# A hybrid decoder trunk in split float32 on one core: low parts of the weights last in every chunk, and the split by whole-chunk instructions on two engines

## The chip, the core and the metric

The kernel runs as one program on one core of a Trainium2 chip. The metric is the device time of one execution in microseconds. Three runs of the kernel before took 1512.72, 1508.36 and 1509.54 us, median 1509.54 us. The rows below come from one further execution that was taken with the hardware profiler.

The engines are named as in the profile: PE is TensorE (matmuls), PEld its weight loads, DVE is VectorE, ACT is ScalarE, POOL is GpSimd, and SP is SyncE, whose queue issues nearly all loads.

## The reference

Two layers on 256 tokens of 1024 channels, in float32:

```python
x = x + pool_mixer(rmsnorm(x), pool_w, pool_scale)          # layer 0
x = x + swiglu(rmsnorm(x), w_gate, w_up, w_down)            # 1024 -> 2816 -> 1024
x = x + ssd_mixer(rmsnorm(x), ...)                          # layer 1: Mamba2 SSD, 2048 inner channels
x = x + moe_swiglu(rmsnorm(x), w_router, ...)               # 8 experts, top 2, 1024 -> 3584 -> 1024
return rmsnorm(x, final_norm_w)

def swiglu(t, w_gate, w_up, w_down):
    return matmul(silu(matmul(t, w_gate)) * matmul(t, w_up), w_down)
```

Nearly all of the bytes are weights, and of these most belong to the eight experts (8 x 3 x 1024 x 3584 float32 numbers).

## The kernel before

**Split products.** A float32 number x is split exactly into a high part `hi` (x rounded to the type float32r) and a low part `lo = x - hi`. A product of two float32 matrices is then three float32r products that accumulate in one PSUM tile: high by high, high by low and low by high. So every weight is used by PE three times as 1024 or 512 columns of moving data: twice as its high part (with the activations' high and low parts) and once as its low part (with the activations' high part).

**The stream of weights.** The class `Stream` holds a list of 404 chunks in the order of their use, almost all of 1 MB (128 partitions x 2048 numbers). Line 80 issues a chunk's load on SP's queue as soon as a unit (a 1 MB buffer) is free. `ahead` splits a chunk: ACT copies it into the high part's unit (line 96), and VectorE subtracts that from the raw chunk into the low part's unit (line 99). Each chunk is split in two halves of 1024 columns, so by two instructions on ACT and two subtractions. `pool_every` gives the second half's subtraction of every n-th chunk to POOL: of every chunk in the pool mixer, of none in the dense SwiGLU, of every second in most of the SSD layer, and of every third from the SSD's output product to the end. `look` says how many chunks ahead of its use a chunk is split: two in most of the kernel, so `next()` of chunk c puts the split of chunk c + 2 into the queues of ACT and DVE, before whatever the program adds there afterwards. Chunks whose weights are scaled by a column (`scale`, the SSD's output product) take lines 102 and 103.

**Stages.** The pool mixer and the start of the dense SwiGLU (0 to about 50 us), the dense SwiGLU (to about 250 us), the SSD layer with the router (to about 490 us), the eight experts (to about 1490 us), and the last scatter and final norm. In the expert stage there are 56 blocks, seven for each expert, and a block takes six chunks: two of the gate product, two of the up product (`gmm`, lines 996 to 998: per chunk 4 k tiles of three products with 512 columns) and two of the down product (`D_part`, which calls `rows_mm`, line 276: per chunk 2 k tiles of six products with 512 columns). Between gate and up stand four transposes (line 1030); line 1011 is the gate's silu on ACT, 1024 the product with the up half on DVE, 238 and 239 the split of the hidden activations. At an expert's end come line 987 (two on DVE) and four additions of line 975, with eight products on PE.

**Order.** The program fixes the order of instructions on each engine by hand (`manual_schedule`); an engine takes its queue in order, so an instruction that waits holds all behind it. The waits are found by the framework from the tiles that an instruction reads and writes.

Of the kernel before, what the change touches and what calls it, by code (L numbers as in the profile page):

```python
# [40 lines left out]
class Stream:  # L41
    """The weights in the order of their use: loads that run ahead as far as free units allow, and
    the exact split of each float32 chunk into two float32r parts a few chunks before its products."""

    def __init__(self, nc, unit, chunks):
# [7 lines left out]
        self.pool_every = 0  # L53
# [30 lines left out]
    def ahead(self, to):  # L84
        while self.ns < min(to, len(self.chunks)):
# [40 lines left out]
def trunk_kernel(ctx, tc, x, cols, bands, cbf, rows, dskip, poolw, dgate, dup, ddown, wdt, wxbc, wz, wout,  # L126
# [114 lines left out]
    def norm(t, w, junk, add):  # L241
        """the residual's update (in halves) and its rmsnorm, for a token tile."""
# [9 lines left out]
    def norm_T(t, junk, th, tl):  # L252
        """the normed token tile transposed and split: [d, k, t] in two parts."""
# [7 lines left out]
    def wst(ps, wh, wl, f, xh, xl, ks):  # L261
        """channel-major product: weights stationary, both token tiles moving."""
        n = len(ks)
        for i, k in enumerate(ks):
# [7 lines left out]
    def rows_mm(acc, lh, ll, wh, wl, start, stop, hs=(0, 1)):  # L272
        """token-major product with one k tile of weights [128, 1024] moving."""
        for a, w, first, last in ((lh, wh, start, False), (lh, wl, False, False), (ll, wh, False, stop)):
            for h in hs:
                mm(acc[h], a, w[:, h * 512:(h + 1) * 512], start=first, stop=last)  # L276
                if between:
                    between.pop(0)()
# [998 lines left out]
```

## Time and profile before

| what | value |
|---|---|
| runs | 1508.36, 1509.54 (median), 1512.72 us |
| span of the profiled execution, first to last instruction | 1505.8 us, 19848 instructions (no time around it is listed) |
| PE busy | 1451.1 us (96%) |
| DVE, ACT, POOL busy | 1235.6 (82%), 1004.9 (67%), 428.0 us (28%) |
| granted TensorE clock, mean | 0.993 |
| read from HBM | 426.45 MB |

A matmul's end is modelled in the profile and matmuls overlap, so PE's busy time is no measure of its best pace; that is read from the distance between the starts of matmuls. An idle row such as `PE a L997 <- DVE u L99: 21.3, 29` means: PE stood idle 21.3 us in 29 places just before a matmul of line 997, and what ended it was DVE's instruction of line 99.

### The profile page before, as it was taken

Reading aid. Unit: us, or ns where it says so; the run is one execution under the profiler, and the core shown is the slowest. Engines: PE = TensorE matmul, PEld = TensorE weight load, DVE = VectorE, ACT = ScalarE, POOL = GpSimd, SP = SyncE. Lnnn points to the kernel's source line nnn. Section 1 sums busy time; section 2 is a strip of 40 time slices with the busy share of each in tenths; the row PEclk is TensorE's granted clock in tenths of the full one; section 3 lists DMA queues with packets and bytes.
Section 4 is the critical chain, followed back from the end, with each engine's and each line's share of the span. In section 5 each row is a group of like instructions: output and inputs, shape, how many; then the busy total and the mean of one; then the engine's idle time right before and its main releaser. Section 6 shows DMA issues by size and latency. Waiting matters only on the chain. (4 is left out here: it accounts for less than half of the span.)

```text
span 1505.8 us, 19848 instructions
## 1 busy us (share of the span) xinstructions
PE 1451.1 (96%) x7533; PEld 1215.1 (81%) x7534; DVE 1235.6 (82%) x1157; ACT 1004.9 (67%) x1248; POOL 428.0 (28%) x208
## 2 busy tenths in 40 slices
PE   7999999899999999999999999999999999999997
PEld 6999989899887787778877787888877777777775
DVE  7554557997767999998888899798898979889996
ACT  6443445766656777776776777777777667767775
POOL 3100004443223343232332333333323222332231
PEclk9999999999999999999999999999999999999998
DMA  8655365424456999888999998899998789999950
GB/s 339 253 184 180 109 240 211 140 79 146 168 203 276 351 360 362 306 334 311 383 360 350 351 342 323 319 368 376 351 351 331 305 348 360 355 343 342 342 211 30
DMA packets 60439, 428.87 MB, mean 285 GB/s; under 512 B 6832, under 2 KB 6960, under 8 KB 9008
## 3 DMA queue, kind: packets, MB, share of 16 engines
q1 hardware_dynamic: 59760, 425.94, 73.7%
q10 hardware_dynamic: 576, 1.59, 0.3%
q8 instruction: 61, 1.00, 0.3%
q14 instruction: 42, 0.34, 0.1%
HBM read 426.45 MB, written 1.05 MB: 284 GB/s over the span
## 5 line engine op out<-in xcount | busy, mean ns | idle before, releaser
L99 DVE TENSOR_TENSOR u<-u 128x1024 fp32r<-128x1024 f32 x665 | 943.2, 1464 | 177.5 <-ACT u L96 109.9
L96 ACT ACTIVATE u<-u 128x1024 fp32r<-128x1024 f32 x789 | 780.5, 1053 | 214.8 <-issue 40.1
L99 POOL TENSOR_TENSOR u<-u 128x1024 fp32r<-128x1024 f32 x124 | 353.2, 2849 | 731.1 <-ACT u L96 441.6
L997 PE MATMUL a<-u 128*128 128x512 f32 x896 | 355.6, 397 | 22.5 <-DVE u L99 21.3
L996 PE MATMUL a<-u 128*128 128x512 f32 x896 | 356.0, 397 | 0.0
L998 PE MATMUL a<-u 128*128 128x512 f32 x896 | 351.8, 393 | 0.0
L276 PE MATMUL b<-u,q 128*128 128x512 f32 x1344 | 319.2, 392 | 3.4 <-DVE u L99 3.4
L276 PEld LDWEIGHTS b<-u,q 128*128 128x128 f32 x1344 | 251.1, 188 | 60.3 <-DVE u L99 6.0
L997 PEld LDWEIGHTS a<-u 128*128 128x128 f32 x896 | 168.5, 188 | 73.7 <-DVE u L99 36.2
L998 PEld LDWEIGHTS a<-u 128*128 128x128 f32 x896 | 168.2, 188 | 36.8
L996 PEld LDWEIGHTS a<-u 128*128 128x128 f32 x896 | 168.3, 188 | 36.0
L266 PE MATMUL b<-u 128*128 128x256 f32 x584 | 166.7, 286 | 3.0 <-ACT u L96 3.0
L268 PE MATMUL b<-u 128*128 128x256 f32 x584 | 166.1, 284 | 1.1 <-DVE u L99 0.9
L267 PE MATMUL b<-u 128*128 128x256 f32 x584 | 165.9, 284 | 0.0
L266 PEld LDWEIGHTS b<-u 128*128 128x128 f32 x584 | 112.7, 193 | 3.9 <-ACT u L96 3.4
L268 PEld LDWEIGHTS b<-u 128*128 128x128 f32 x584 | 112.6, 193 | 1.5 <-DVE u L99 1.5
L267 PEld LDWEIGHTS b<-u 128*128 128x128 f32 x584 | 112.8, 193 | 0.5
L1011 ACT ACTIVATE q<-a,s 128x512 f32<-128x512 f32 x56 | 38.4, 685 | 55.5 <-PE a L998 55.5
L276 PE MATMUL a<-u,q 128*128 128x512 f32 x264 | 62.1, 391 | 0.7 <-ACT q L238 0.7
L276 PEld LDWEIGHTS a<-u,q 128*128 128x128 f32 x264 | 48.8, 188 | 10.6 <-ACT q L238 0.9
L597 DVE SCALAR_TENSOR_TENSOR q<-pad,col,q 128x256 f32<-128x256 f32 x96 | 55.3, 641 | 0.2
L515 POOL TENSOR_SCALAR nega<-nega 128x1 f32<-128x1 f32 x1 | 0.2, 245 | 192.6 <-ACT nega L514 192.6
(262 smaller groups left out, 1124.9 us busy)
## 6 DMA issues: line engine op xcount, KB each, us to landing
u<-in_mgate SPq DMA_DIRECT2D x112, 1024.0 KB, 6.9
u<-in_mup SPq DMA_DIRECT2D x112, 1024.0 KB, 6.9
u<-in_mdown SPq DMA_DIRECT2D x111, 1024.0 KB, 6.7
u<-in_wxbc SPq DMA_DIRECT2D x16, 1024.0 KB, 4.8
u<-in_dgate SPq DMA_DIRECT2D x11, 1024.0 KB, 4.9
u<-in_dup SPq DMA_DIRECT2D x11, 1024.0 KB, 7.3
u<-in_ddown SPq DMA_DIRECT2D x11, 1024.0 KB, 4.8
u<-in_wz SPq DMA_DIRECT2D x8, 1024.0 KB, 4.8
```

The lines of the kernel that those rows point to most:

```text
L96: self.nc.scalar.activation(hi[:, c], raw[:, c], AF.Copy)
L99: eng.tensor_sub(lo[:, c], raw[:, c], hi.bitcast(F32)[:, c])
L266: mm(ps, wh[:, k, c], xh[:, k], start=i == 0, stop=False)
L267: mm(ps, wh[:, k, c], xl[:, k], start=False, stop=False)
L268: mm(ps, wl[:, k, c], xh[:, k], start=False, stop=i == n - 1)
L276: mm(acc[h], a, w[:, h * 512:(h + 1) * 512], start=first, stop=last)
L515: pool.tensor_scalar(nega, nega, -1.0, None, op0=ALU.mult)
L597: dve.scalar_tensor_tensor(r[:, c], pad[:, c, 1 + k:1 + k + T], w[c][k], r[:, c], op0=ALU.mult, op1=ALU.add)
L996: mm(ps, a, wh[:, k], start=i == 0 and k == 0, stop=False)
L997: mm(ps, a, wl[:, k], start=False, stop=False)
L998: mm(ps, b, wh[:, k], start=False, stop=i == 1 and k == 3)
L1011: act(sil, ps, AF.Silu, scale=pair[e // 2].g[:, e % 2, 1:2])
```

## The change

Two things change together. First, in `wst`, `rows_mm`, `z_tile` and `gmm` the products with the high part of a chunk's weights come first for all k tiles of the chunk, and those with the low part last. `rows_mm` now takes all k tiles of a chunk at once, and `by_half` applies to a whole chunk. Second, an unscaled chunk is split by one instruction of 2048 columns on ACT and one on DVE; `pool_every` goes away, and with it POOL's part in the split. Line numbers in the new file are one to four lower or up to five higher.

```diff
             hi, lo = self.get([P, n], F32R), self.get([P, n], F32R)
-            for p, s in enumerate(range(0, n, D)):
-                c = slice(s, s + D)
-                if scale is None:
-                    self.nc.scalar.activation(hi[:, c], raw[:, c], AF.Copy)
-                    on_pool = p == 1 and self.pool_every and i % self.pool_every == 0
-                    eng = self.nc.gpsimd if on_pool else self.nc.vector
-                    eng.tensor_sub(lo[:, c], raw[:, c], hi.bitcast(F32)[:, c])
-                else:
-                    w = scale[s // D]
+            if scale is None:
+                self.nc.scalar.activation(hi, raw, AF.Copy)
+                self.nc.vector.tensor_sub(lo, raw, hi.bitcast(F32))
+            else:
+                for p, s in enumerate(range(0, n, D)):
+                    c, w = slice(s, s + D), scale[p]
...
-        for i, k in enumerate(ks):
-            c = slice(f * P, (f + 1) * P)
             mm(ps, wh[:, k, c], xh[:, k], start=i == 0, stop=False)
             mm(ps, wh[:, k, c], xl[:, k], start=False, stop=False)
+        for i, k in enumerate(ks):
             mm(ps, wl[:, k, c], xh[:, k], start=False, stop=i == n - 1)
...
+    def rows_mm(acc, tiles, start, stop, by_half=False):
+        n = len(tiles)
+        ops = []
+        for i, (lh, ll, wh, wl) in enumerate(tiles):
+            ops += [(lh, wh, start and i == 0, False), (ll, wh, False, False)]
+        for i, (lh, ll, wh, wl) in enumerate(tiles):
+            ops.append((lh, wl, False, stop and i == n - 1))
+        for hs in ((0,), (1,)) if by_half else ((0, 1),):
+            for a, w, first, last in ops:
+                for h in hs:
+                    mm(acc[h], a, w[:, h * 512:(h + 1) * 512], start=first, stop=last)
...
             for k in range(4):
-                a, b = pr.h[:, 4 * i + k, s], pr.l[:, 4 * i + k, s]
-                mm(ps, a, wh[:, k], start=i == 0 and k == 0, stop=False)
-                mm(ps, a, wl[:, k], start=False, stop=False)
-                mm(ps, b, wh[:, k], start=False, stop=i == 1 and k == 3)
+                mm(ps, pr.h[:, 4 * i + k, s], wh[:, k], start=i == 0 and k == 0, stop=False)
+                mm(ps, pr.l[:, 4 * i + k, s], wh[:, k], start=False, stop=False)
+            for k in range(4):
+                mm(ps, pr.h[:, 4 * i + k, s], wl[:, k], start=False, stop=i == 1 and k == 3)
...
-    st.reserve, st.look, st.pool_every = 2, 2, 3
+    st.reserve, st.look = 2, 2
```

On PE, in one chunk of an expert's gate product before (u_5499 and u_5500 are the chunk's high and low parts, u_4545 and u_4546 the activations' high and low parts):

```order
L996 MATMUL a_5519<-u_5499,u_4545 128x512 [waits Activation_49]
L997 MATMUL a_5519<-u_5500,u_4545 128x512 [waits DVE_49]
L998 MATMUL a_5519<-u_5499,u_4546 128x512
...
L996 MATMUL a_5519<-u_5499,u_4545 128x512 [waits Activation_49]
L997 MATMUL a_5519<-u_5500,u_4545 128x512 [waits Pool_49]
L998 MATMUL a_5519<-u_5499,u_4546 128x512
```

The first low part is read by the chunk's second product, that of the second half by its eighth. The same place in the changed kernel (u_6245 and u_6246 are the chunk's parts, u_5884 and u_5885 the activations'):

```order
L995 MATMUL a_6263<-u_6245,u_5884 128x512 [waits Activation_49]
L996 MATMUL a_6263<-u_6245,u_5885 128x512
...
L995 MATMUL a_6263<-u_6245,u_5884 128x512
L996 MATMUL a_6263<-u_6245,u_5885 128x512
L998 MATMUL a_6263<-u_6246,u_5884 128x512 [waits DVE_49]
L998 MATMUL a_6263<-u_6246,u_5884 128x512 x3
```

The one wait on the low part has moved from the chunk's second product to its ninth, and the wait on POOL is gone.

On DVE, in an expert block before, from the product with the up half on (each u is a chunk's low part, raw chunk and high part):

```order
L1024 SCALAR_TENSOR_TENSOR q_6887<-a_6898,s41_6459,q_6887 128x512 [waits PE_49]
L99 TENSOR_TENSOR u_6941<-u_6638,u_6940 128x1024 [waits DMAHW2_49,PE_49,Activation_49]
L99 TENSOR_TENSOR u_6941<-u_6638,u_6940 128x1024 [waits Activation_49]
L99 TENSOR_TENSOR u_6961<-u_6664,u_6960 128x1024 [waits DVE_49,DMAHW3_49,PE_49,Activation_49]
L99 TENSOR_TENSOR u_6982<-u_6684,u_6981 128x1024 [waits DMAHW4_49,PE_49,Activation_49]
L99 TENSOR_TENSOR u_6982<-u_6684,u_6981 128x1024 [waits Activation_49]
L99 TENSOR_TENSOR u_7002<-u_6713,u_7001 128x1024 [waits DMAHW5_49,PE_49,Activation_49]
L99 TENSOR_TENSOR u_7002<-u_6713,u_7001 128x1024 [waits Activation_49]
L239 TENSOR_TENSOR q_7029<-b_7023,q_7028 128x512 [waits Activation_49]
```

The chunk of u_6961 has one half here; its other half is in POOL's queue. The same stretch of a block in the changed kernel:

```order
L1024 SCALAR_TENSOR_TENSOR q_6131<-a_6185,s40_4580,q_6131 128x512 [waits PE_49]
L94 TENSOR_TENSOR u_6224<-u_5963,u_6223 128x2048 [waits DMAHW0_49,DVE_49,Activation_49]
L94 TENSOR_TENSOR u_6246<-u_5977,u_6245 128x2048 [waits DMAHW1_49,DVE_49,Activation_49]
L94 TENSOR_TENSOR u_6265<-u_5995,u_6264 128x2048 [waits DMAHW2_49,PE_49,Activation_49]
L94 TENSOR_TENSOR u_6283<-u_6037,u_6282 128x2048 [waits DMAHW3_49,PE_49,Activation_49]
L235 TENSOR_TENSOR q_6308<-b_6302,q_6307 128x512 [waits Activation_49]
```

Seven half-chunk subtractions on DVE, and one on POOL, have become four whole-chunk ones on DVE.

On DVE at the kernel's start, the split of the pool mixer's weights before (u_163, u_98 and u_162 are their low part, raw chunk and high part; q and a, b are the mixer's activations):

```order
L314 SCALAR_TENSOR_TENSOR u_109<-xs_75,s7_141,u_108 128x512 [waits Activation_49] x2
L99 TENSOR_TENSOR u_163<-u_98,u_162 128x1024 [waits DMAHW3_49,Activation_49]
L353 SCALAR_TENSOR_TENSOR q_209<-a_168,col_76,q_208 128x256 [waits DMAHW4_49,Activation_49]
L353 SCALAR_TENSOR_TENSOR q_209<-b_169,col_76,q_208 128x256 [waits Activation_49]
L353 SCALAR_TENSOR_TENSOR q_215<-a_170,col_76,q_214 128x256 [waits Activation_49]
```

And in the changed kernel:

```order
L319 SCALAR_TENSOR_TENSOR u_109<-xs_75,s7_141,u_108 128x512 [waits Activation_49] x2
L94 TENSOR_TENSOR u_163<-u_98,u_162 128x2048 [waits DMAHW3_49,Activation_49]
L358 SCALAR_TENSOR_TENSOR q_207<-a_166,col_76,q_206 128x256 [waits DMAHW4_49,Activation_49]
L358 SCALAR_TENSOR_TENSOR q_207<-b_167,col_76,q_206 128x256 [waits Activation_49]
L358 SCALAR_TENSOR_TENSOR q_213<-a_168,col_76,q_212 128x256 [waits Activation_49]
```

The eight instructions on the mixer's activations now stand behind a subtraction of twice the length.

## Rows read from the trace of the kernel before

**Rows 1.** Busy time by stage. Columns: stretch in us from the span's start, its length, busy us and instructions of PE, PEld, DVE, ACT and POOL, granted TensorE clock, share of the DMA engines' time, GB/s.

```profile
0.00:50.00 50.00, 41.75 (x281) 36.40 (x282) 34.31 (x55) 30.76 (x53) 17.82 (x15) 0.93 0.86 340
50.00:250.00 200.00, 198.61 (x1370) 184.74 (x1369) 109.21 (x116) 90.70 (x115) 4.78 (x13) 1.00 0.52 188
250.00:500.00 250.00, 243.06 (x1563) 213.94 (x1562) 199.13 (x265) 161.22 (x274) 95.24 (x72) 0.99 0.47 175
500.00:1000.00 500.00, 488.51 (x2195) 394.22 (x2195) 451.37 (x362) 364.78 (x405) 159.67 (x55) 1.00 0.89 346
1000.00:1440.00 440.00, 424.54 (x1899) 342.62 (x1898) 390.85 (x317) 314.72 (x350) 134.90 (x48) 1.00 0.90 346
```

**Rows 2.** Who waited for whom, PE alone, whole execution: us in total, number of times, longest.

```profile
PE a L997 <- DVE u L99: 21.3, 29, 1.7
PE b L257 <- DVE u L250: 4.2, 3, 2.3
PE b L276 <- DVE u L99: 3.4, 6, 1.2
PE b L266 <- ACT u L96: 3.0, 1, 3.0
...
PE a L997 <- POOL u L99: 1.1, 3, 0.6
...
PE b L268 <- DVE u L99: 0.9, 1, 0.9
```

**Rows 3.** The instructions in order of time around one of those waits, 1097 to 1101 us. Columns: start us, us, engine, line, operation and tiles, count, and the idle time before with what ended it.

```profile
1096.17 5.69 DVE L99 TENSOR_TENSOR u<-u 128x1024 fp32r<-128x1024 f32 x3
...
1097.03 2.62 POOL L99 TENSOR_TENSOR u<-u 128x1024 fp32r<-128x1024 f32 x1 [4.79 <-PE b L276]
1097.10 0.39 PE L996 MATMUL a<-u 128*128 128x512 f32 x1
...
1099.82 0.39 PE L996 MATMUL a<-u 128*128 128x512 f32 x1
...
1100.79 0.50 PE L997 MATMUL a<-u 128*128 128x512 f32 x1 [0.58 <-DVE u L99]
```

**Rows 4.** ACT's splits in the same stretch, in order of time.

```profile
1092.27 2.02 ACT L96 ACTIVATE u<-u 128x1024 fp32r<-128x1024 f32 x2 [1.12 <-POOL u L99]
1094.49 2.01 ACT L96 ACTIVATE u<-u 128x1024 fp32r<-128x1024 f32 x2 [0.20 <-DVE u L99]
```

**Rows 5.** The half-chunk subtraction on DVE, shortest, median and longest in ns, and its first and last start: first in 500 to 1490 us, where POOL has a share, then in 50 to 200 us, where it has none.

```profile
L99 DVE TENSOR_TENSOR u<-u x543: 1205/1217/3445, 498.2 to 1486.7; 128x1024 fp32r<-128x1024 f32 x181
```

```profile
L99 DVE TENSOR_TENSOR u<-u x55: 1217/1221/1229, 49.9 to 195.9; 128x1024 fp32r<-128x1024 f32 x55
```

**Rows 6.** DVE's groups of instructions in 500 to 1440 us: busy us, mean ns of one, idle time before them and what ended it.

```profile
L99 DVE TENSOR_TENSOR u<-u 128x1024 fp32r<-128x1024 f32 x516 | 749.9, 1500 | 95.3 <-ACT u L96 37.2 <-PE a L997 26.8 <-PE a L998 13.7
L1024 DVE SCALAR_TENSOR_TENSOR q<-a,s,q 128x512 f32<-128x512 f32 x51 | 37.7, 740 | 0.0
L239 DVE TENSOR_TENSOR q<-b,q 128x512 fp32r<-128x512 f32 x51 | 34.8, 682 | 0.2
L987 DVE SCALAR_TENSOR_TENSOR q<-b,s,q 128x512 fp32r<-128x512 f32 x14 | 9.8, 740 | 0.2 <-ACT q L986 0.2
L975 DVE TENSOR_TENSOR xs<-xs,a 128x512 f32<-128x512 f32 x14 | 9.5, 680 | 0.0
```

**Rows 7.** The half-chunk subtractions alone, 500 to 1440 us: length, busy us and count on DVE, then on POOL, granted clock, DMA share and GB/s.

```profile
500.00:1440.00 940.00, 747.53 (x516) 294.57 (x103) 1.00 0.89 346
```

**Rows 8.** ACT's half-chunk copy and its copy of 512 columns, whole execution: busy us, mean ns | idle before.

```profile
L96 ACT ACTIVATE u<-u 128x1024 fp32r<-128x1024 f32 x789 | 780.5, 1053 | 214.8 <-issue 40.1 <-DVE u L99 39.6 <-PE a L997 35.4
...
L238 ACT ACTIVATE q<-b 128x512 fp32r<-128x512 f32 x57 | 33.7, 591 | 5.4 <-PE b L470 3.7 <-PE b L1030 1.7
```

**Rows 9.** The kernel's start in order of time: ACT, DVE and POOL.

```profile
10.19 1.99 ACT L96 ACTIVATE u<-u 128x1024 fp32r<-128x1024 f32 x2
...
12.57 0.48 DVE L353 SCALAR_TENSOR_TENSOR q<-a,col,q 128x256 fp32r<-128x256 f32 x1
...
21.66 1.22 DVE L99 TENSOR_TENSOR u<-u 128x1024 fp32r<-128x1024 f32 x1
22.07 6.39 POOL L99 TENSOR_TENSOR u<-u 128x1024 fp32r<-128x1024 f32 x2 [7.34 <-ACT u L96]
22.80 1.28 DVE L239 TENSOR_TENSOR u<-b,u 128x512 fp32r<-128x512 f32 x2
24.07 2.13 DVE L99 TENSOR_TENSOR u<-u 128x1024 fp32r<-128x1024 f32 x1
26.12 0.68 DVE L376 TENSOR_TENSOR qa<-a,row 128x512 f32<-128x512 f32 x1
26.83 2.18 DVE L383 TENSOR_TENSOR xs<-xs,qa 128x512 f32<-128x512 f32 x1
28.93 0.68 DVE L376 TENSOR_TENSOR qa<-a,row 128x512 f32<-128x512 f32 x1
```

**Rows 10.** PE at the same time: the last matmul before its wait for the second token tile's norm, and the wait.

```profile
30.12 0.28 PE L412 MATMUL b<-u 128*128 128x256 f32 x1
32.74 0.53 PE L257 MATMUL b<-col,u 128*128 128x128 f32 x2 [2.34 <-DVE u L250]
```

More of the change, by code (lines that the diff above doesn't have):

```diff
@@ L263, in wst @@
         n = len(ks)
+        c = slice(f * P, (f + 1) * P)
         for i, k in enumerate(ks):
-            c = slice(f * P, (f + 1) * P)
             mm(ps, wh[:, k, c], xh[:, k], start=i == 0, stop=False)
             mm(ps, wh[:, k, c], xl[:, k], start=False, stop=False)
+        for i, k in enumerate(ks):
             mm(ps, wl[:, k, c], xh[:, k], start=False, stop=i == n - 1)
     between = []
[L272 to L278, printed above, removed]
+    def rows_mm(acc, tiles, start, stop, by_half=False):
[9 more added lines that the diff above has]
+                    mm(acc[h], a, w[:, h * 512:(h + 1) * 512], start=first, stop=last)
+                    if between:
+                        between.pop(0)()
     def finish(src):
@@ L436, in down @@
         for t in ts:
-            for hs in ((0,), (1,)) if f == NFD - 1 else ((0, 1),):
-                for c in range(2):
-                    l = slice(t * P, (t + 1) * P)
-                    rows_mm(acc[t], parts[0][:, c, l], parts[1][:, c, l], dh[:, c], dl[:, c],
-                            f == 0 and c == 0, f == NFD - 1 and c == 1, hs)
+            l = slice(t * P, (t + 1) * P)
+            rows_mm(acc[t], [(parts[0][:, c, l], parts[1][:, c, l], dh[:, c], dl[:, c]) for c in range(2)],
+                    f == 0, f == NFD - 1, f == NFD - 1)
         if w is None:
@@ L445, in trunk_kernel @@
     parts = []
-    st.look, st.pool_every = 2, 0
+    st.look = 2
     for f in range(NFD):
@@ L603, in z_tile @@
         for k in range(4):
-            a, b = th[:, 4 * i + k, l], tl[:, 4 * i + k, l]
-            mm(zps[t], a, wh[:, k], start=i == 0 and k == 0, stop=False)
-            mm(zps[t], a, wl[:, k], start=False, stop=False)
-            mm(zps[t], b, wh[:, k], start=False, stop=i == 1 and k == 3)
+            mm(zps[t], th[:, 4 * i + k, l], wh[:, k], start=i == 0 and k == 0, stop=False)
+            mm(zps[t], tl[:, 4 * i + k, l], wh[:, k], start=False, stop=False)
+        for k in range(4):
+            mm(zps[t], th[:, 4 * i + k, l], wl[:, k], start=False, stop=i == 1 and k == 3)
     def z_chunk(zps, i):
@@ L738, in trunk_kernel @@
                 next(dtg)
-                st.pool_every = 2
             step(j - 2)
@@ L803, in out_proj @@
         yh, yl = yT[o // 4]
+        k = [(2 * o + e) % 8 for e in range(2)]
         for t in ts:
             l = slice(t * P, (t + 1) * P)
-            for hs in ((0,), (1,)) if by_half else ((0, 1),):
-                for e in range(2):
-                    k = (2 * o + e) % 8
-                    rows_mm(acc[t], yh[:, k, l], yl[:, k, l], wh[:, e], wl[:, e],
-                            o == 0 and e == 0, o == 7 and e == 1, hs)
+            rows_mm(acc[t], [(yh[:, k[e], l], yl[:, k[e], l], wh[:, e], wl[:, e]) for e in range(2)],
+                    o == 0, o == 7, by_half)
         if w is None:
@@ L1037, in D_part @@
         dh, dl = st.next(n)
-        for k in range(n):
-            kk = 2 * i + k0 + k
-            last = b % NFB == NFB - 1 and kk == 3
-            for hs in ((0,), (1,)) if last else ((0, 1),):
-                rows_mm(acc, hh[:, kk], hl[:, kk], dh[:, k], dl[:, k], b % NFB == 0 and kk == 0, last, hs)
+        kk = [2 * i + k0 + k for k in range(n)]
+        last = b % NFB == NFB - 1 and kk[-1] == 3
+        rows_mm(acc, [(hh[:, kk[k]], hl[:, kk[k]], dh[:, k], dl[:, k]) for k in range(n)],
+                b % NFB == 0 and kk[0] == 0, last, last)
         st.done()
```

4 lines of the change are left out of this document (2 added, 2 removed).

## The prediction

> **What bounds the kernel now.** I read busy time by stage first, then PE's waits, then the timeline around one wait, then the durations of the split. By stage [rows 1] PE is busy 198.6 of 200 us in the dense layer, 243.1 of 250 in the SSD layer, and 488.5 + 424.5 of 940 us from 500 to 1440, at the full granted clock. So PE sets the time nearly everywhere, and what can be won without fewer products is what it waits: 27 us visible in those 940. PE's waits [rows 2] name the splits: lines 997, 276 and 268 waited for a low part 29 + 6 + 3 + 1 = 39 times, 21.3 + 3.4 + 1.1 + 0.9 = 26.7 us. DVE is the next engine, 451.4 + 390.9 = 842 us of the same 940, 90%.
>
> The timeline [rows 3] shows what makes a low part late. POOL's subtraction starts at 1097.03 and takes 2.62 us; the three of DVE that begin at 1096.17 take 5.69 us, where three of 1.22 us would take 3.6; and PE's second product of the chunk starts at 1100.79, ended by DVE. The durations [rows 5] say the same of the stage: median 1217 ns, longest 3445 ns, and where POOL has no share 1217 to 1229 ns without exception. So a subtraction on DVE that meets one on POOL loses up to 3.45 - 1.22 = 2.2 us. In 500 to 1440 us the mean is 1.500 us [rows 6], which is (1.500 - 1.217) x 516 = 146 us lost, for 103 halves that POOL took over [rows 7]: 1.42 us lost for each, more than the 1.22 us that DVE would have needed to do it itself.
>
> The Trainium skill ("Perfetto Trace Analysis", section "Optimizing Scalar/DVE Operations") has two sentences that speak against the change: with a saturated DVE, offloading to GpSimd may make sense, and where an engine is not saturated but causes bubbles, "breaking up instructions may allow work to be completed sooner". It adds that VectorE and GpSimd share a read port, so that offloading between them might not help. The trace agrees with the last by the 1.42 us; the rule on breaking up is taken up as the second case below.
>
> **Products in a new order.** PE's instructions are the same in number and size. Starts from 1097.10 to 1099.82 [rows 3] are 12 products of three kinds in 2.72 us, 0.227 us each, whether the stationary operand is that of the product before (997 after 996) or another; so I cost the order itself at nothing. What it moves is the time at which the low part must be there: from the second product to the ninth for a first half, 7 x 0.227 = 1.6 us later, and from the eighth to the ninth for a second half, 0.2 us later.
>
> **Whole-chunk split.** On ACT 512 columns take 0.591 us and 1024 take 1.053 [rows 8], so 2048 take 1.053 + 2 x 0.462 = 1.98 us; two halves together take 2.01 [rows 4], so ACT's load does not change. On DVE 512 columns take 0.680 [rows 6], 1024 take 1.217 [rows 5], so 2048 take 1.217 + 2 x 0.537 = 2.29 us (between 2.15, with no fixed part at all, and 2.43, two halves). From 500 to 1440 us there are (516 + 103) / 2 = 309.5 chunks: 709 us, and DVE's other groups are 842 - 748 = 94 us, so 803 us. Against about 910 us that remain for the stretch that is 88%: DVE, with POOL's share taken back, has less to do than before. POOL's queue holds nothing else that anything in this stage waits for. The DMA engines move 346 GB/s at a share of 0.89 to 0.90 [rows 1]; in 910 us they would need 346 x 940 / 910 = 357, a share of 0.92. That leaves them as cover.
>
> **Does the low part then come in time?** For the chunk in [rows 3] the split's pair on ACT is the one that starts at 1094.49 [rows 4], 5.3 us ahead of the chunk's first product at 1099.82. One copy ends at 1096.47, one subtraction at 1098.8, and the ninth product is due at 1099.82 + 8 x 0.227 = 1101.6: 2.9 us to spare, or 0.6 us if DVE is still busy with a whole chunk when the copy ends. So in the steady run I take all 39 waits as gone.
>
> **What they cost.** A wait's row understates it: the product at 1100.79 was due at 1099.82 + 0.227 = 1100.05, so 0.74 us were lost where the row says 0.58, since the modelled 0.39 us of the matmul before it hide 0.39 - 0.23 = 0.16. So 26.7 + 39 x 0.16 = 33 us go.
>
> **What is late next.** At an expert's end DVE gets two instructions of 0.740 and four of 0.680 us in a lump [rows 6], 4.2 us; the eight products of that place give PE 8 x 0.227 = 1.8 us to do, so the splits behind are 2.4 us later against PE. That lies within 2.9 and exceeds 0.6 by 1.8. With the hidden 0.16, eight ends cost between 0 and 16 us. I take 3: five ends with the mean of line 276's waits, 3.4 / 6 = 0.57.
>
> **The start.** Here POOL's help is lost on a path that PE waits for. The whole subtraction starts when the whole copy ends, 10.19 + 1.98 = 12.17, and ends at 14.46; line 353, which begins at 12.57 [rows 9], begins 1.9 us later. Further on, the two halves at 21.66 and 24.07 become whole ones: the next instructions started 1.14 and 2.05 us after them, and will start about 2.25 after, so 1.1 and 0.2 later. Back comes that line 383 at 26.83 took 2.18 us under POOL and kept line 376 until 28.93, 2.10 us, where 0.65 will do: 1.45 earlier. In sum 1.9 + 1.1 + 0.2 - 1.45 = 1.7 us later for PE's wait at 32.74 [rows 10]. PE's products before it ended near 30.4 and shift by up to 3 us, still inside that wait. I count 1.7 us; nothing (if the 2.34 us wait covers it after all) and 4 us (if PE's clock, 0.93 here [rows 1], stays low longer) are the bounds. In the SSD layer POOL's halves move to DVE as well; PE's one long wait there, 3.0 us of line 266 on ACT [rows 2], gets up to 0.93 longer, since a whole copy ends 1.98 - 1.05 later than a first half, and the 0.9 of line 268 in the sum above may go. I leave both inside the bounds.
>
> **Sum.** -33 + 1.7 + 3 = -28.3 us on a span of 1505.8, so 1477.5. The median of the runs is 3.7 us above that span, which I take as what lies around it and carry over: 1481 us.
>
> **The rivals.**
> Forecast: the waits go, 1481. Its own range is 1472 (no new waits, nothing at the start, and the 4 us by which the runs scatter) to 1490.
> Second: the coarser split brings back waits at the places where DVE is lumped. For it: a whole copy ends 0.93 us after the first half did, and DVE is 88% taken. Against: the place of need moves by 1.6 us. Price: the upper bound of the eight ends, 16 in place of 3, so 1494.
> Third: the place of the wait moves and its length stays: PE's first product now needs the whole high part, and units come free no earlier. For it: ACT waits for PE to give back a unit, 35.4 us in all for line 997 alone [rows 8]. Against: only one wait for ACT's split in the whole execution [rows 2]. The 33 us come back: 1509 to 1514, no change.
> Fourth, slower: the subtraction is slow for another reason than POOL (traffic of loads, say), and DVE becomes the bound. It decides from (910 - 94) / 309.5 = 2.64 us for a whole chunk; at twice the mean of [rows 6], 3.00 us, DVE needs 309.5 x 3.00 + 94 = 1023, 113 us more than PE: 1481 + 113 = 1594. Against it: the shortest and the median, 1205 and 1217 ns, are found in the same stage, under the same loads.
>
> **How the numbers follow.** Forecast 0.79, second 0.12, third 0.05, fourth 0.04. About 0.3%, 4.5 us, is what a measurement can tell from no change. Forecast and second are faster by more than that, 0.91; the third is the same, 0.05; the fourth slower, 0.04. The range runs from 1471 to 1496, the forecast's own range and the second case's 1494, with the rest outside.
>
> **What would show it.** In the changed profile: POOL has no subtraction of line 99's kind left; line 94 on DVE reads 2.2 to 2.4 us with no long ones; waits of PE on it are under 5 us in all; products keep 0.227 us; PE's wait at the norm near 33 us is still there, later. It is wrong if PE's idle time in the experts stays above 15 us, if line 94 has a mean over 2.6 us, or if line 995 waits for ACT.

## The result, and the profile after

The changed kernel took 1477.02 us (median of four runs, 1474.85 to 1477.93), the kernel before 1510.44 us on the same chip (1508.36 to 1512.72). The ratio is 0.978, with a 95% interval of 0.976 to 0.980. The profiled execution took 1477.93 us and has a span of 1476.1 us, 29.7 us less than before.

Busy time by stage of the changed kernel, with the columns of [rows 1]; the last stretch ends at 1410 us, since the program ends earlier:

```profile
0.00:50.00 50.00, 41.33 (x263) 34.60 (x264) 34.48 (x52) 28.48 (x46) 3.34 (x10) 0.93 0.82 322
...
250.00:500.00 250.00, 243.35 (x1552) 215.01 (x1551) 185.06 (x245) 154.56 (x244) 65.73 (x62) 0.96 0.45 168
500.00:1000.00 500.00, 499.23 (x2267) 409.56 (x2266) 438.32 (x263) 359.94 (x246) 0.00 (x0) 1.00 0.92 356
1000.00:1410.00 410.00, 409.87 (x1860) 337.59 (x1860) 360.92 (x213) 295.51 (x200) 0.00 (x0) 1.00 0.93 362
```

In the experts PE is now busy 499.2 of 500 us, where it was 488.5 [rows 1]. DVE has 438.3 us there, 88%. One number stands out: the granted clock of 250 to 500 us fell from 0.99 to 0.96.

PE's waits, as in [rows 2] (us in total, times, longest):

```profile
PE b L262 <- ACT u L93: 3.5, 1, 3.5
PE a L365 <- DVE q L358: 2.5, 1, 2.5
...
PE a L799 <- DVE q L792: 1.5, 1, 1.5
PE b L416 <- DVE u L94: 1.4, 1, 1.4
...
PE b L265 <- DVE u L94: 0.6, 1, 0.6
...
PE a L998 <- DVE u L94: 0.4, 2, 0.2
...
PE a L995 <- ACT u L93: 0.3, 1, 0.3
```

The 39 waits of 26.7 us for low parts are down to 0.4 + 0.6 = 1.0 us in three places (lines 998 and 265; line 281 has none), and one that the kernel before did not have is new, 1.4 us of line 416 at the start. Line 365's wait there and line 799's are longer than those of the same products before (0.7 us of line 360, 1.0 of line 797). The split itself, in 500 to 1440 us (shortest, median and longest in ns), and then its groups in the whole execution (busy us, mean ns):

```profile
L94 DVE TENSOR_TENSOR u<-u x322: 2277/2286/2295, 500.2 to 1436.9; 128x2048 fp32r<-128x2048 f32 x161
```

```profile
L94 DVE TENSOR_TENSOR u<-u 128x2048 fp32r<-128x2048 f32 x396 | 892.0, 2280 | 206.3 <-ACT u L93 188.9
L93 ACT ACTIVATE u<-u 128x2048 fp32r<-128x2048 f32 x396 | 743.8, 1908 | 195.9 <-PE b L281 64.8
```

The longest subtraction is 9 ns above the median; before, it was 2.2 us above it [rows 5]. Four rows of a steady place, in order of time, answer to [rows 3]:

```profile
1095.77 4.49 DVE L94 TENSOR_TENSOR u<-u 128x2048 fp32r<-128x2048 f32 x2
1095.91 0.39 PE L995 MATMUL a<-u 128*128 128x512 f32 x1
...
1097.05 0.39 PE L996 MATMUL a<-u 128*128 128x512 f32 x1
...
1097.27 1.07 PE L998 MATMUL a<-u 128*128 128x512 f32 x4
```

PE goes from the last product with the high part (1097.05) to the four with the low part (1097.27) in 0.22 us and without an idle time, while DVE works on later chunks.

**Where the time went.** The stages can be cut at matmuls that both programs have, read from the starts in the timeline. Before: the norm's transposes at 32.74 [rows 10], the SSD's last channel-major product of a high part with a high part (393.83; the row after it is the last of all), the first expert product and the last output product:

```profile
393.83 0.28 PE L266 MATMUL b<-u 128*128 128x256 f32 x1
...
394.07 0.28 PE L268 MATMUL b<-u 128*128 128x256 f32 x1
...
468.32 0.39 PE L996 MATMUL a<-u 128*128 128x512 f32 x1
...
1487.73 3.58 PE L276 MATMUL b<-u,q 128*128 128x512 f32 x15
```

The last row is a group of 15 products, and its last one starts at 1490.93. In the changed kernel the four cuts are at 35.73, 394.87, 476.12 and 1460.93.

| stage | before | after | difference |
|---|---|---|---|
| start, to the norm's transposes | 32.74 | 35.73 | +3.0 |
| dense layer and SSD, to the second cut | 361.09 | 359.14 | -1.9 |
| SSD's output product, router, scatter | 74.49 | 81.25 | +6.8 |
| experts | 1022.61 | 984.81 | -37.8 |
| last additions, final norm | 14.9 | 15.1 | +0.3 |

The second cut does not divide the work alike. Before, two products of that chunk follow it, the last one at 394.07; in the new order nine do, the last eight of them in this row, and the last of all at 395.95:

```profile
395.11 1.12 PE L265 MATMUL b<-u 128*128 128x256 f32 x8
```

So 0.8 us of the second and third row only changed sides. For the same work the SSD's stage gained 1.1 us, and the next one lost 5.9 (80.17 after 74.25).

The experts gave more than the whole result, and 5.9 us were lost in a stage that the prediction did not look at. There PE ran at half its clock. The same columns as above, first before, 455 to 465 us, and then after, 455 to 475 us:

```profile
455.00:460.00 5.00, 4.62 (x32) 3.55 (x32) 4.54 (x8) 3.01 (x7) 3.60 (x3) 0.95 1.01 424
460.00:465.00 5.00, 4.60 (x21) 1.99 (x20) 3.70 (x14) 1.78 (x3) 1.48 (x2) 0.70 0.90 346
```

```profile
455.00:460.00 5.00, 5.00 (x20) 4.43 (x19) 0.74 (x2) 0.00 (x0) 0.00 (x0) 0.50 1.02 429
460.00:465.00 5.00, 5.00 (x20) 4.04 (x20) 3.57 (x8) 2.40 (x6) 2.56 (x2) 0.50 1.02 423
465.00:470.00 5.00, 5.00 (x18) 3.13 (x19) 3.14 (x11) 1.64 (x4) 2.82 (x4) 0.50 0.08 30
470.00:475.00 5.00, 5.00 (x34) 3.56 (x33) 2.16 (x4) 2.13 (x5) 0.00 (x0) 0.79 0.31 105
```

0.50 is 1.2 of 2.4 GHz. Before, the half clock lasted 5 x (0.05 + 0.30) / 0.5 = 3.5 us; after, 15 + 5 x 0.21 / 0.5 = 17.1 us.

These are two single executions, and the clock differs from one execution to the next. The mean granted clock of 40 others of the kernel before is on record: it lies between 0.986 and 0.994, with a median of 0.989. The nine executions at 0.992 or more took 1507.3 to 1510.6 us, the thirteen at 0.988 or less 1511.7 to 1513.8 us. The profiled one has 0.993, and its span of 1505.8 us is shorter than that of 39 of the 40. The nine executions of the changed kernel have 0.986 to 0.990. So the kernel before, too, mostly runs at a lower mean clock than its profile shows, in stretches that no profile names, and how much of the 17.1 us the change brought is not shown.

PE's timeline there shows what came ahead (the router's products, line 799, alternate with the output product's, line 281):

```profile
452.26 0.48 PE L281 MATMUL b<-u 128*128 128x512 f32 x1
454.25 0.39 PE L799 MATMUL a<-col,q 128*128 128x8 f32 x2 [1.51 <-DVE q L792]
...
455.73 0.77 PE L281 MATMUL b<-u 128*128 128x512 f32 x1
...
456.58 0.77 PE L281 MATMUL b<-u 128*128 128x512 f32 x1
```

In the changed kernel PE stands 1.51 us until DVE has copied the transposed residual, and about a microsecond later the same pair of products takes 0.85 us (455.73 to 456.58).

### The profile page after: what moved, and what is told of

Its sections match the earlier page's. It is cut to its first block, busy times and chain, and to the rows that moved or that the text cites. A ratio compares the mean times of both kernels' runs of the same rounds, so it can differ in the third digit from the quotient of the medians.

```text
span 1476.1 us, 18694 instructions
## 1 busy us (share of the span) xinstructions
PE 1446.1 (98%) x7534; PEld 1223.5 (83%) x7534; DVE 1174.3 (80%) x888; ACT 968.1 (66%) x855; POOL 74.1 (5%) x84
## 5 line engine op out<-in xcount | busy, mean ns | idle before, releaser
L94 DVE TENSOR_TENSOR u<-u 128x2048 fp32r<-128x2048 f32 x396 | 892.0, 2280 | 206.3 <-ACT u L93 188.9
L93 ACT ACTIVATE u<-u 128x2048 fp32r<-128x2048 f32 x396 | 743.8, 1908 | 195.9 <-PE b L281 64.8
L995 PE MATMUL a<-u 128*128 128x512 f32 x896 | 356.2, 398 | 0.3 <-ACT u L93 0.3
L996 PE MATMUL a<-u 128*128 128x512 f32 x896 | 351.9, 393 | 0.0
L998 PE MATMUL a<-u 128*128 128x512 f32 x896 | 242.9, 393 | 0.4 <-DVE u L94 0.4
L262 PE MATMUL b<-u 128*128 128x256 f32 x584 | 145.0, 286 | 3.5 <-ACT u L93 3.5
L263 PE MATMUL b<-u 128*128 128x256 f32 x584 | 144.3, 284 | 0.0
L262 PEld LDWEIGHTS b<-u 128*128 128x128 f32 x584 | 112.6, 193 | 4.4 <-ACT u L93 3.9
L263 PEld LDWEIGHTS b<-u 128*128 128x128 f32 x584 | 112.8, 193 | 0.5
L265 PE MATMUL b<-u 128*128 128x256 f32 x584 | 82.4, 284 | 0.6 <-DVE u L94 0.6
L265 PEld LDWEIGHTS b<-u 128*128 128x128 f32 x584 | 75.7, 193 | 0.8 <-DVE u L94 0.8
L281 PE MATMUL b<-u 128*128 128x512 f32 x192 | 50.6, 412 | 0.2 <-ACT u L234 0.2
```

Of the source, the lines that this page charges most:

```text
L93: self.nc.scalar.activation(hi, raw, AF.Copy)
L94: self.nc.vector.tensor_sub(lo, raw, hi.bitcast(F32))
L995: mm(ps, pr.h[:, 4 * i + k, s], wh[:, k], start=i == 0 and k == 0, stop=False)
L996: mm(ps, pr.l[:, 4 * i + k, s], wh[:, k], start=False, stop=False)
L998: mm(ps, pr.h[:, 4 * i + k, s], wl[:, k], start=False, stop=i == 1 and k == 3)
```

## The experiments

Twelve kernels were run, always beside the kernel before on the same chip; the ratios go by that. In the tables "stage" is the routing stage, from the second cut above to the first expert product (with the new order it holds 0.8 us more of the SSD's products than with the old one), and "experts" goes from there to the last output product.

**1. The two halves of the change, and POOL alone.** The first kernel has only the new order (the split as before: halves, with POOL's share). The second has only the whole-chunk split without POOL. The third takes the kernel before and sets POOL's share to nothing:

```diff
-    st.look, st.pool_every = 4, 1
+    st.look, st.pool_every = 4, 0
...
-                st.pool_every = 2
+                st.pool_every = 0
...
-    st.reserve, st.look, st.pool_every = 2, 2, 3
+    st.reserve, st.look, st.pool_every = 2, 2, 0
```

> The new order of products alone; the split as before, in halves, with POOL's share. Theory (low parts are late where DVE stands behind POOL, by 0.2 to 1.6 us; the order gives first halves 1.6 us more, second halves 0.2): nearly all waits of first halves go, those of second halves stay, in all 3 to 6 us of the 27 us; nothing is lost at the start; DVE's longest subtraction stays 3.4 us. 1478 to 1486 us. Rival (DVE is simply full, and the order only moves the waits): DVE is at 842 us of 910, the waits come back, 1495 or more.

> Whole-chunk instructions on ACT and DVE, no POOL; the products in the old order, so the low part is due at the chunk's second product. Theory: no subtraction over 2.3 us; in the steady run the low part is 1.3 us early or, behind a whole chunk, 1.0 us late; waits of some 5 to 12 us come at the experts' ends, plus 3 us at the start: 1484 to 1494 us. Rival (the order is what cured the waits): most of the waits stay, 1500 us or more. Other rival (POOL's removal is all): under 1480.

> Only POOL's share goes to DVE: halves as before, old order. Theory: all subtractions take 1.2 us, DVE has 619 x 1.22 + 95 = 850 us of 910 to do from 500 to 1440 us, first halves are early, waits of low parts 3 to 8 us in all: 1480 to 1488 us. Rival (order or whole-chunk instructions made the gain): within 0.5% of before, 1503 or more.

| kernel | median us | ratio (95%) | stage | experts |
|---|---|---|---|---|
| before | 1511.81 | 1 | 74.5 | 1022.6 |
| order alone | 1485.97 | 0.983 (0.981 to 0.985) | 75.3 | 999.2 |
| whole-chunk split alone | 1498.72 | 0.993 (0.990 to 0.995) | 79.1 | 1006.6 |
| POOL's share alone taken away | 1472.60 | 0.974 (0.972 to 0.976) | 78.2 | 984.4 |
| changed kernel | 1477.02 | 0.978 (0.976 to 0.980) | 81.3 | 984.8 |

The subtraction on DVE in 500 to 1440 us and PE's largest wait for it, order alone:

```profile
L99 DVE TENSOR_TENSOR u<-u x529: 1206/1214/3449, 499.2 to 1439.9; 128x1024 fp32r<-128x1024 f32 x177
```

```profile
PE a L1003 <- DVE u L99: 4.7, 10, 0.9
```

The split alone:

```profile
L95 DVE TENSOR_TENSOR u<-u x315: 2278/2291/2295, 499.1 to 1438.8; 128x2048 fp32r<-128x2048 f32 x158
```

```profile
PE a L994 <- DVE u L95: 13.7, 18, 1.3
PE b L273 <- DVE u L95: 3.4, 5, 1.0
```

POOL's share alone taken away:

```profile
L99 DVE TENSOR_TENSOR u<-u x642: 1212/1220/1229, 499.9 to 1439.0; 128x1024 fp32r<-128x1024 f32 x161
```

With the new order the long subtractions are still there (3449 ns), and PE waits for fewer of them: the order forgives them, and they stay. In all 8.2 us of waits for low parts are left of 26.7, more than the 3 to 6 expected. Without POOL there is not one above 1229 ns in the same stage, under the same loads, though DVE does all the work. This alone brings 38.2 us in the experts, as much as both parts of the change together, so POOL's share was nearly the whole cost there; the new order on top of it (experiment 4) brings another 2.0. The split alone shows what its coarseness costs in the old order: no subtraction is long, yet PE waits for it 23 times in the experts, 17.1 us, because the second product already needs a low part that takes 2.29 us. In the changed kernel the order covers that. The second kernel ended 5 us above its expected range, the third 7 us below its own: halves on DVE alone were better, and whole chunks in the old order worse, than the theory had it.

**2. Is it POOL, or POOL's reading?** Two kernels add work on POOL alone to the changed kernel: at every third chunk of the experts a copy of one column of the high part (so that POOL starts where it did before), then four instructions of 256 columns. In one they are subtractions that read SBUF, in the other memsets that only write; the output does not depend on them.

```diff
+                if self.junk is not None and i % 3 == 0:
+                    self.nc.gpsimd.tensor_copy(self.junk[:, :1], hi.bitcast(F32)[:, :1])
+                    for _ in range(4):
+                        self.nc.gpsimd.tensor_sub(self.junk, self.other[:, :256], self.other[:, 258:514])
```

In the second, the last line is `memset(self.junk, 0.0)`.

> The changed kernel with work added on POOL that no one waits for: in the experts, at every third chunk, one copy of one column (so that POOL waits for ACT's part) and four subtractions of 256 columns that read two SBUF tiles and write a tile of their own. Theory (POOL's subtractions hold up DVE's): DVE's whole-chunk subtraction, 2.28 to 2.30 us at its longest in the changed kernel, has cases of 3 us and more; low parts have 2 us and more to spare, so PE's waits stay under 8 us and the time within 1476 to 1486 us. Rival (DVE's long ones before were due to something else): no subtraction over 2.4 us.

> As the run before, but POOL's four instructions are memsets of 256 columns, which read nothing. If it is POOL's reads of SBUF that hold up DVE: no subtraction on DVE over 2.4 us, time as the changed kernel, 1475 to 1479 us. If any work on POOL does: longer ones as in the run before.

Measured: 1524.16 us with the reads, ratio 1.007 (1.004 to 1.009), and 1475.37 us with the writes, ratio 0.976 (0.975 to 0.978), as the changed kernel. Of the kernel with reads, durations in 500 to 1440 us of DVE's subtraction, POOL's subtraction and POOL's copy of one column:

```profile
L95 DVE TENSOR_TENSOR u<-u x306: 2274/2386/2732, 500.0 to 1438.9; 128x2048 fp32r<-128x2048 f32 x153
```

```profile
L99 POOL TENSOR_TENSOR junk<-col x405: 634/2567/2785, 500.1 to 1439.1; 128x256 f32<-128x256 f32 x135
```

```profile
L97 POOL COPY junk<-u x101: 183/2127/2347, 511.0 to 1436.9; 128x1 f32<-128x1 f32 x101
```

Of the kernel with writes, DVE's subtraction and POOL's memset:

```profile
L95 DVE TENSOR_TENSOR u<-u x322: 2278/2286/2296, 500.2 to 1439.7; 128x2048 fp32r<-128x2048 f32 x161
```

```profile
L99 POOL MEMSET junk<- x428: 312/313/321, 502.6 to 1433.0; 128x256 f32 x143
```

Beside memsets DVE is as it is alone. Beside reads both engines lose: a POOL subtraction that takes 0.63 us undisturbed has a median of 2.57, so it stood behind one of DVE's 2.29 us, and DVE loses up to 2.73 - 2.29 = 0.45 us at a time. Even one column read by POOL takes 0.18 or 2.13 us, and in the trace every such copy of over 1.5 us ends 41 to 46 ns after the end of one of DVE's subtractions. The copies of one column stand in the kernel with the writes too; beside them and the memsets DVE's longest is 2.296 us. The Trainium skill ("SBUF — State Buffer", section "Who interferes with whom") says that a VectorE instruction with two SBUF inputs contends with a GpSimd instruction that reads SBUF and not with one that only writes it; it calls the shared pair of ports an exclusive lock, and says that issue order decides who blocks. Both kernels agree, by these numbers. The time of the kernel with reads is no measure of what DVE loses, since ACT's copies waited for POOL's reading of their units' column (us in total, times, longest):

```profile
ACT u L94 <- POOL junk L97: 58.8, 18, 6.6
```

The expected 3 us for the longest subtraction and the expected time both missed, and so did the 8 us for PE's waits: line 1003 alone waited 11.2 us for ACT's copies.

**3. The half clock of the routing stage.** First the changed kernel once more; then one in which the router's products start four products later (empty slots between); then one in which six bf16 products of 512 columns into a tile that nothing reads stand where PE waits:

```diff
-    between += parts
+    between += [lambda: None] * 4 + parts
```

```diff
+    fill = pa()
+
+    def warm_fill():
+        for _ in range(6):
+            mm(fill, cb[:, B_ID:B_ID + P], cb[:, :512], start=True, stop=True)
+
-    between += parts
+    between += [warm_fill] + parts
```

> The changed kernel once more, beside the next three on the same chip. 1475 to 1479 us; granted clock at half for 14 to 17 us in the routing stage.

> The changed kernel; the router's eight small products start four products later within the last output product, so PE has 0.9 us more to do before it needs DVE's copy of the transposed residual (line 792). Theory (PE's wait of 1.5 us there is what brings TensorE's clock to half for 17 us, against 3.4 us before the change): the wait falls to about 0.6 us, the half clock to 0 to 4 us, the out-projection and routing get 4 to 7 us shorter: 1470 to 1474 us. Rival (the stage is longer for another reason, DVE's whole-chunk subtraction ahead of the residual): 1476 to 1477 us, and the clock as in the changed kernel.

> The changed kernel with six bf16 products of 512 columns into a tile that nothing reads (extra work on PE, nothing left out), put right behind the first half of the last chunk's output product, where PE waits 1.5 us for the copy of the transposed residual ahead of the router's products. Theory (the clock falls because PE stands idle there): the half clock in 450 to 475 us, 17.1 us in the changed kernel and 13.7 in its second profile, falls to 3.4 us or less, the routing stage from 80 or 81 to 75 to 78 us, 1470 to 1474. Rival (the clock falls for what comes later, the router's products of 8 columns and their waits, or by chance): 10 us or more at half clock, 1476 to 1479.

| kernel | median us (range) | ratio (95%) | wait ahead of the router | half clock, us | stage |
|---|---|---|---|---|---|
| changed, again | 1477.71 (1475.02 to 1477.83) | 0.977 (0.975 to 0.978) | 1.48 | 13.7 | 79.9 |
| four slots | 1475.95 (1474.52 to 1476.29) | 0.976 (0.975 to 0.977) | 0.54 | 3.4 | 77.7 |
| filled | 1472.82 (1472.30 to 1472.97) | 0.974 (0.973 to 0.976) | 0 | 0 | 76.4 |

The slots shortened the wait and the half clock, and part of it came back as new waits of 1.0 and 1.2 us further on. The time missed the 1470 to 1474 us that the theory gave, and the mean clock of its five runs, 0.989 and once 0.990, is not above the changed kernel's. In the kernel with the filling products PE's timeline at the same place reads:

```profile
452.10 0.48 PE L281 MATMUL b<-u 128*128 128x512 f32 x1
452.42 1.47 PE L867 MATMUL a<-cb 128*128 128x512 bf16 x5
453.53 0.58 PE L281 MATMUL b<-u 128*128 128x512 f32 x1
454.06 0.39 PE L799 MATMUL a<-col,q 128*128 128x8 f32 x2
```

(the profile has five of the six filling products) and the clock of the next stretch, where the changed kernel has 0.50:

```profile
455.00:460.00 5.00, 4.71 (x29) 3.54 (x28) 2.80 (x6) 1.42 (x5) 1.37 (x2) 1.00 1.01 426
```

The router's products start at 454.06 in place of 454.25, so the filling itself moves nothing; the clock stays at 1.00 to the experts, the stage is 3.5 to 4.9 us shorter than in the changed kernel's two profiles, and the median is 4.2 and 4.9 us lower. The interval of the ratio (0.9730 to 0.9757) lies below that of the changed kernel's first runs (0.9761 to 0.9796) and just touches that of the second (from 0.9754). The mean clock is 0.993 in each of its five runs, where the changed kernel's nine have 0.986 to 0.990. So the half clock costs 4 to 5 us, and PE's idle time there takes part in it. Not all that the clock gives back is kept: PE now waits 1.2 us at line 906 and 0.5 at line 956, which the changed kernel does not. That the idle time is the only condition is not shown: the kernel with memsets had the same wait of 1.51 us and only 3.4 us of half clock in its profile (that of its fastest run, 1472.44 of up to 1477.07), the kernel before 0.97 us and 3.5, and POOL's share alone taken away 0.97 us and 13.7. The whole-chunk split alone has 1.74 us and 13.7, the order alone 0.70 us and none.

**4. Halves, the new order, and no POOL.** One kernel combines the new order with half-chunk instructions on ACT and DVE alone (the diff below with `on_pool` never true, and the silu as it was). Three more add to it: POOL for the second half of the very first chunk, a silu moved behind the chunk after it, and the four slots; the same without the slots; and the same without the slots and with the filling products.

```diff
-            if scale is None:
-                self.nc.scalar.activation(hi, raw, AF.Copy)
-                self.nc.vector.tensor_sub(lo, raw, hi.bitcast(F32))
-            else:
...
+            for p, s in enumerate(range(0, n, D)):
+                c = slice(s, s + D)
+                if scale is None:
+                    self.nc.scalar.activation(hi[:, c], raw[:, c], AF.Copy)
+                    on_pool = p == 1 and i == 0
+                    eng = self.nc.gpsimd if on_pool else self.nc.vector
+                    eng.tensor_sub(lo[:, c], raw[:, c], hi.bitcast(F32)[:, c])
...
-            act(X[i], X[i], AF.Silu)
+            if i:
+                act(X[0], X[0], AF.Silu)
+                act(X[1], X[1], AF.Silu)
```

> The new order of products with halves on ACT and DVE, and no POOL: the third single step undone. Theory (with POOL gone the low parts are early, so the order has nothing left to save): within 2 us of the kernel with halves on DVE in the old order, 1471 to 1475 us. Rival (order adds to it): under 1470 us.

> New order, halves on ACT and DVE; POOL only for the second half of the very first chunk; the four empty slots ahead of the router's products; the silu of an SSD chunk pair behind the split of the next chunk. Theory: against halves with the new order 4 to 7 us from the clock, 3 us from line 266's wait for ACT in the SSD layer, about 1 us at the start: 1461 to 1466 us. If the clock's stretch has another cause: 1468 to 1470 us.

> The kernel with the new order, halves on ScalarE and VectorE alone, POOL for the second half of the very first chunk only, and the silu of the first token tile behind the chunk of the second, without the four empty slots. Theory (the four slots brought the half clock back into the routing stage, 10.2 us of it, and the start is 2 us earlier for the other two edits): routing stage 75 to 76 us as with the new order and halves alone (75.3), no half clock there, 1463 to 1465. Rival (the half clock there hangs on when the stage begins, or on chance, not on the slots): 3.4 us or more at half clock in 450 to 475 us, routing stage 77 us or more, 1466 to 1468.

> The last version (new order, halves on ScalarE and VectorE alone, POOL for the second half of the very first chunk, the silu moved) with the six filling products of the run before it; the products are extra work on PE, nothing is left out. Theory (any idle time of PE in the routing stage can bring the half clock, and the last version's 3.4 us of it came behind two later waits of 1.3 and 0.5 us): the wait ahead of the router's products is only 0.7 us in that version, where the filling products take 1.3 us, so they cost up to 0.6 us; the half clock behind the later waits may stay: 1465 to 1468, within 0.2% of the last version. Rival (it is the wait ahead of the router's products alone that decides): no half clock in the stage, 1463 to 1465.

| kernel | median us | ratio (95%) | norm's transposes | half clock, us | stage | experts |
|---|---|---|---|---|---|---|
| order and halves | 1467.07 | 0.971 (0.969 to 0.972) | 35.05 | 0 | 75.3 | 982.4 |
| with all three additions | 1465.89 | 0.970 (0.968 to 0.971) | 32.98 | 10.2 | 77.5 | 982.3 |
| without the slots | 1466.90 | 0.970 (0.968 to 0.971) | 34.05 | 3.4 | 76.8 | 982.3 |
| filled, without the slots | 1467.09 | 0.971 (0.970 to 0.972) | 33.76 | 0 | 76.2 | 982.3 |

All four are 10 to 12 us below the changed kernel, and their intervals overlap: which of them is best is not settled. For the first kernel the rival came: against halves without POOL in the old order (1472.60 us, on another chip) the new order brings 5.5 us more, 2.0 of them in the experts and most of the rest in the routing stage, where 13.7 us of half clock fell to none. The second kernel's time lies at the upper end of its range, and not by its theory: the half clock is there, and while line 266's wait for ACT fell from 3.0 to 0.3 us, 3.1 us of line 269's waits for DVE came in its place. As far as one profile each can tell, the four slots did bring the half clock (10.2 us against 3.4 without them), as the theory of the third kernel had it, but its 1463 to 1465 us did not come. In the fourth kernel the rival's clock came (none at half) and not its time. The expert stage of the first:

```profile
469.00:1410.00 941.00, 940.60 (x4271) 773.16 (x4270) 849.86 (x822) 707.77 (x788) 0.00 (x0) 1.00 0.91 356
```

PE is busy 940.6 of 941 us, so in this stage nothing is left to win by an earlier split. Against the second run of the changed kernel, on the same chip, halves are 10.6 us faster. By their two profiles (1475.8 and 1466.3 us of span): 2.6 us up to the SSD's last channel-major product, 4.6 in the routing stage, where 13.7 us of half clock fell to none, and 2.4 in the experts.

## Why the prediction was right, and where it was not

The time, 1477, is 4 us below the forecast of 1481 and inside its own range. As a span the forecast was 1477.5, only 1.4 us above the 1476.1 measured, and that closeness is luck. For the same work in each stage, the experts came out 7.8 us better than the sum had them (-37.8 in place of -33 + 3) and the SSD 1.1 us, the routing stage 5.9 us worse, the start 1.3 and the end 0.3.

- **POOL as the cause of the late low part.** Right, and shown: without POOL the long subtractions are gone, whatever the order; with POOL's reads they come back, with its writes not. The fourth rival fell with the first view: line 94 has a longest of 2.295 us, far from its 2.64.
- **All 39 waits gone, -33 us.** Right in kind: 1.0 us of 26.7 is left (and 1.4 us of line 416 came new at the start), and line 268's 0.9 stayed as line 265's 0.6, as the prediction had left open. In the experts 37.8 us went. Counted from the starts of the 4456 matmuls of that stage against the pace of 0.227 us, 42 distances of over 0.45 us held 34.4 us before, and 6 hold 2.2 now: that is the term of 33. What it left out are short ones, of 0.26 to 0.45 us, which the waits' rows hardly show: 109 with 10.9 us before, 66 with 6.1 now, another 4.8 us.
- **Durations.** DVE's 2.29 us was measured as 2.286, its 88% as 438.3 of 500 us, DMA's 0.92 as 0.92 and 0.93. ACT's whole copy took 1.908, not 1.98: the second 1024 columns added 0.855 us and not twice the 0.462 of the step from 512 to 1024.
- **What is late next, +3 us at eight expert ends.** Wrong: line 998 waited 0.4 us in two places. The spare time of 2.9 us holds, the 0.6 us with DVE in the middle of a whole chunk did not decide. With that the second rival fell too; the Trainium skill's sentence on breaking up instructions, which it had been taken from ("Perfetto Trace Analysis", section "Optimizing Scalar/DVE Operations"), did not decide by that mechanism, but it holds for the whole: in the new order without POOL, halves beat whole chunks by 10.6 us, of which 4.6 lie where the clock differs too.
- **The start, +1.7 us.** It measured +3.0 in this profile, inside the bounds of 0 and 4, and +4.5 in the second one (37.23), just outside. What the prediction worked out held, and the clock came on top. DVE's rows, the first answering to line 353 of [rows 9]:

```profile
12.31 2.29 DVE L94 TENSOR_TENSOR u<-u 128x2048 fp32r<-128x2048 f32 x1 [1.00 <-ACT u L93]
14.52 0.48 DVE L358 SCALAR_TENSOR_TENSOR q<-a,col,q 128x256 fp32r<-128x256 f32 x1
...
18.74 0.88 DVE L385 SCALAR_TENSOR_TENSOR qa<-a,col,row 128x256 f32<-128x256 f32 x2 [0.99 <-PE a L375]
```

Line 358 began at 14.52 in place of 12.57, the 1.9 us that were predicted. PE, which had waited for it, then ran at a lower clock:

```profile
15.05 1.44 PE L365 MATMUL a<-qa 128*128 128x512 bf16 x3 [2.46 <-DVE q L358]
...
16.72 0.41 PE L375 MATMUL a<-u,q 128*128 128x256 f32 x1
16.93 0.41 PE L373 MATMUL a<-u,q 128*128 128x256 f32 x1
...
18.18 0.28 PE L373 MATMUL a<-u,q 128*128 128x256 f32 x1
18.30 0.28 PE L374 MATMUL a<-u,q 128*128 128x256 f32 x1
```

A product of 256 columns takes 0.21 us to the next until about 18 us, then 0.12 (the granted clock of 14 to 19 us is 0.66, before it was 1.00), and DVE's line 385 waited 0.99 us for it: 1.9 and 1.0 are the whole 3.0. That the longer wait brought the low clock is not shown, and two kernels speak against it. With the order alone PE waits 0.7 us there, as before, and yet the clock of 14 to 19 us is 0.68, DVE waits as long, and the norm's transposes come at 34.32:

```profile
17.26 0.88 DVE L389 SCALAR_TENSOR_TENSOR qa<-a,col,row 128x256 f32<-128x256 f32 x2 [1.10 <-PE a L379]
```

With the whole-chunk split alone PE waits 2.5 us, the clock there stays at 1.00, DVE does not wait, and the transposes come at 34.35. So the split by itself costs 1.6 us at the start, near the 1.7 of the sum, and a low clock at that place about 1 us more, with or without the split. With halves, POOL's part in the first chunk and the moved silu together gave back 1.0 to 2.1 us of the start (32.98 to 34.05 in three profiles against 35.05); one alone was not tried, and the clock differs here too (1.00 in 14 to 19 us for the 32.98, 0.66 for the 35.05).
- **The SSD layer.** Line 262's wait for ACT went from 3.0 to 3.5 us, within the 0.93 allowed. The stage still gained 1.1 us for the same work, which had no term in the sum.
- **The sum's silent step.** The prediction had no term for the routing stage; it took it as unchanged, and 5.9 us went there between the two profiles. Nearly all of it goes with the clock: in the kernel with the filling products, which has no half clock there, the stage takes 75.31 us for the same work, 1.1 more than before. [Rows 1] gave its 250 to 500 us one clock of 0.99, and the first stretch's low clock was the only one that the prediction weighed. This is the step that failed: the clock of one execution, 0.993, was taken for the kernel's, where the median of 40 is 0.989. The experts' larger gain hid it in the span, and whether the change itself lowers the clock there stays open. Between the medians, whose clocks are alike, the change brought 33.4 us, 5 more than the sum's 28.3.
- **From the span to the median.** The prediction carried 3.7 us over. In the runs of the changed kernel the time is 1.7 to 1.9 us above the same run's span; the rest was the distance between the profiled execution before and its median. Here the median lies 0.9 us above the profiled span, since this profile is that of the slowest of four runs. That is 2.8 of the 4 us by which the forecast was high.

The third rival (the wait moves to the high part) fell with line 995's single wait of 0.3 us.

## What to carry to other kernels

Before giving an engine a share of another's work, look at the longest against the median duration of what stays behind: here POOL's help made DVE's instruction cost 1.42 us more for each 1.22 us that it took over, and taking the help away was worth as much as the whole change. A coarser split and a later need cancel each other (984.8 us in the experts with both, 984.4 with neither), so make one without the other in an experiment before keeping both; the fine split in the new order is the best kernel found. And cut the time by stages at fixed instructions, with the same work on both sides, even when the total comes out as forecast; before a span is taken as the base, see whether the profiled execution's clock is that of the others.

## What the runs showed that was not expected

- A stretch at half TensorE clock near 455 us came and went with edits elsewhere: 17.1 and 13.7 us in two profiles of one kernel, 0 to 13.7 us in the others, at a price of 4 to 5 us for the longest. With PE's wait there filled by products the clock did not fall in either of the two kernels tried, and the five runs of the changed kernel with it lie within 0.7 us, where the changed kernel's own lie 3 us apart. That a kernel's runs scatter with their clock is shown by the 40 executions of the kernel before; that it is this stretch that differs between them is suggested, and not shown.
- The contention between DVE's two-input subtraction and POOL's reads goes both ways and counts whole instructions: POOL's copy of a single column took 0.18 us or 2.13.
